# A chunked RWKV-7 scan: transition matrices and corrected receptances made ahead of the chain, y evicted once for four chunks

## The chip, the cores and the metric

One core of one Trainium2 chip. The engines are TensorE (PE, with its weight loads as PEld), VectorE (DVE), ScalarE (ACT), GpSimd (POOL) and SyncE (SP), which here only issues DMAs. The metric is the device time of one launch in microseconds (us), as the median of several runs.

## The reference, cut to what matters

The program is a two-layer trunk over 1280 tokens (a prompt of 256 and a sample of 1024) with 1024 channels. Layer 0 mixes tokens by a bidirectional RWKV-7 recurrence, layer 1 by neighbourhood attention, and each is followed by an MLP. The change is in the recurrence of layer 0 alone, which runs for 16 heads of 64 channels, forwards and backwards, and whose two results are added:

```python
def step(S, inp):
    r_t, w_t, k_t, v_t, a_t, b_t = inp
    sa = jnp.einsum('bhvk,bhk->bhv', S, a_t)
    S = S * w_t[:, :, None, :] + sa[..., None] * b_t[:, :, None, :] + v_t[..., None] * k_t[:, :, None, :]
    return S, jnp.einsum('bhvk,bhk->bhv', S, r_t)
...
for d in range(2):
    ...
    y = y + _wkv_scan(rf, _heads(decay), k_d, vf, -kk, kk * iclr, reverse=(d == 1))
```

Behind it y is normalised per token and head, scaled, given a bonus term, gated and projected.

## The kernel before, in words

**Stages.** The kernel first makes the projections and the scaled operands of the scan (`l0_proj`, `prep_*`), which it stores in DRAM as `ar_d` (a and r), `bk_d` (b and k) and `v_d`. Then comes the scan, then layer 0's output and MLP, attention, and layer 1's MLP. All products of the scan are in float32; all others that matter for the time are split into two float32r halves.

**Chunks.** The scan works in chunks of 64 tokens. Two heads lie side by side in the 128 partitions, so every small product is issued by `pair` (L971) as two 64x64 products, one for each half of the array. A pair whose output lies in the partitions that its operands lie in is called straight here; one whose output goes to the other half (`half(1 - e)`) is called crossed.

**Jobs.** A job is 16 chunks of one pair of heads (the sample), or four chunks of each of four pairs (the prompt, in the first two of the ten jobs). It is scanned forwards (d = 0) and backwards (d = 1) at once, so in each of 16 time units a job makes one step for each direction. Its chunks are prepared in eight groups of four (`order` in `scan_job`), one group each two units.

**Preparation of a job**, in this order, with times in units of the job:
- `load`, `prod`, `store` (L798 to L820): a group's `ar` and the b half of `bk` come in, one product gives the matrix `zb` (PSUM tile aps), DVE masks it (L813), and its left half goes to DRAM (`dd`, L816).
- `mload`, `mtr`, `rank1`, `qst`, `qld` (L823 to L889): the diagonal 32x32 blocks of all 32 matrices of the job come back (`mt`, `mraw`, L831), ACT transposes half of them (L840), DVE inverts them all together by 31 rank-1 updates of two instructions (L851, L853), and the result goes to DRAM (`qd`, L864 and L868) and back into `Q` (the program's name is qq, L884) and `qx` (L889). The updates are put over ten units, by an estimate of their cost.
- `merge1`, `merge2` (L895 to L910): the 64x64 inverses are completed from the 32x32 ones (PSUM tiles yps and qps, ACT copies to yt and qq).
- `kload`, `kprod`, `kmask`, `ktr` (L913 to L942): `bk` comes in, one product and DVE's mask (L926) give `zk`, and two transposes per chunk (PSUM tile lps) give `lt`.

**A step of the chain** (`scan_step`, L976) is four pieces at t - 0.68, t, t + 0.33 and t + 0.66. The state S of the chunk before enters a product into w, ACT copies that to `up` (L993), a product with Q gives u, which ACT copies too (L1007), a product with u completes the new state, and ACT scales that by the decay into the new S (L1015). Beside it three products make the chunk's y in the PSUM tile yo, which DVE copies or adds into y after each step (L1019, L1021). So the chain of a step is three products and three copies on ACT. For each direction there is one bank with w, u and the new state (wu) and one for yo.

**After the steps** of a group pair, `scan_post` normalises y, adds the bonus, transposes (PSUM tile zps) and stores it.

**Order.** PE, DVE, ACT and POOL run in an order written out by hand: each piece of work is put in a list with its time (`at`), and the list is sorted. An engine's instructions are then issued in that order, and an instruction that waits holds up all behind it on its engine. SP's DMAs follow an order that the framework makes, near to that of the list; a DMA that waits holds up those behind it as well. A job's preparation starts at `T0` = -34 units, so two further jobs are being prepared while one is scanned: rank-1 updates of the next job run beside the steps of this one.

**Rings.** 20 buffers each of `ar` and `zb` (10 in pool er, which is opened early, and 10 in rp), 4 of bb, 3 each of `bk`, `zk` and `lt`, and 4 PSUM banks (tag aps) that all the prepared products share.

Of the kernel before, what the change touches and what calls it, by code (L numbers as in the profile page):

```python
# [13 lines left out]
P = 128  # L14
# [34 lines left out]
class Trunk:  # L49
# [654 lines left out]
    def scan_begin(self):  # L704
# [9 lines left out]
                                           (("bb", 4, L), ("ar", 10, P), ("zb", 10, P)))  # L714
# [17 lines left out]
    def scan(self):  # L732
# [12 lines left out]
        grow(self.r_ar, rp, "ar", [P, 4, P], 10)  # L745
        grow(self.r_zb, rp, "zb", [P, 4, P], 10)
# [5 lines left out]
        self.pbank = [[self.pw.tile([P, n], F32, name=f"{x}{d}") for x, n in (("wu", 3 * L), ("yo", L))] for d in range(2)]  # L752
# [26 lines left out]
    def scan_job(self, j):  # L779
# [4 lines left out]
        J = {"ar": {}, "zb": {}, "zk": {}, "lt": {}}  # L784
# [3 lines left out]
        T0 = -34.0  # L788
# [4 lines left out]
        for n, (d, g) in enumerate(order):  # L793
# [78 lines left out]
        def qld():  # L872
# [6 lines left out]
            for d in range(2):  # L879
                for b in range(2):  # L880
                    o = 64 * d + 32 * b
                    for e in range(2):
                        q0 = 64 * e + 32 * b
                        nc.sync.dma_start(Q[q0:q0 + 32, :, d, 32 * b:32 * b + 32], J["qd"][d, o:o + 32].rearrange("(c e) s t -> e s c t", e=2)[e])  # L884
# [7 lines left out]
        for n, (d, g) in enumerate(order):  # L892
            m, c0 = grp[g]

            def merge1(d=d, g=g):  # L895
                zb, qx, lo = J["zb"][d, g], J["qx"][d], 32 * d
                yps = self.pt.tile([P, 4, 32], F32, name="yps", tag="aps")
                for c in range(4):
                    self.pair(lambda e, z: (yps[z, c, :], zb[z, c, 0:64], qx[z, 4 * g + c, :]))
                yt = J["yt", d, g] = self.nxt(self.r_yt[d])  # L900
                nc.scalar.copy(yt[:, :, lo:lo + 32], yps)

            def merge2(d=d, g=g):
                Q, yt, hi = J["Q"], J["yt", d, g], 32 - 32 * d
                qps = self.pt.tile([P, 4, 32], F32, name="qps", tag="aps")
                for c in range(4):
                    self.pair(lambda e, z: (qps[z, c, :], yt[z, c, :], Q[z, 4 * g + c, d, hi:hi + 32]))
                nc.scalar.copy(Q[:, 4 * g:4 * g + 4, d, hi:hi + 32], qps)
            t = 2 * n - 3.992
            at(t + 0.52, merge1)  # L910
            at(t + 1.30, merge2)

# [4 lines left out]
            def kprod(c, d=d, g=g):  # L917
                bk, ar = J["bk", d, g], J["ar"][d, g]
                if c == 0:
                    J["pk"] = self.pa.tile([P, 4, P], F32, name="kps", tag="aps")  # L920
                ps = J["pk"]
                self.pair(lambda e, z: (ps[z, c, :], bk[z, c, 64:128], ar[z, c, :]))

            def kmask(d=d, g=g, ps=None):
                zk = J["zk"][d, g] = self.rp.tile([P, 4, P], F32, name="zk", tag="zk", bufs=3)
                nc.vector.tensor_tensor(out=zk, in0=J["pk"], in1=self.mask[d].unsqueeze(1).to_broadcast([P, 4, P]), op=ALU.mult)  # L926

            def ktr(c, d=d, g=g):
                bk = J["bk", d, g]
                if c == 0:  # L930
                    J["pl"] = self.pt.tile([P, 4, 2, L], F32, name="lps", tag="aps")
                ps = J["pl"]
                for i in range(2):
                    self.pair(lambda e, z: (ps[z, c, i, :], bk[z, c, 64 * i:64 * i + 64], self.ident[z, z]))
                if c == 3:
                    lt = J["lt"][d, g] = self.rp.tile([P, 4, 2, L], F32, name="lt", tag="lt", bufs=3)
                    nc.scalar.copy(lt, ps)
            at(t - 1.9, kload)
            at(t + 1.25, kmask)
# [13 lines left out]
        at(-5.423, vload)  # L953
# [5 lines left out]
        for d in range(2):  # L959
            for i in range(16):  # L960
# [4 lines left out]
                self.scan_step(at, i + 0.481 * d, J, st[d], d, cc, m, c0 + cc % 4, new, end, i >= 8, j == len(self.jobs) - 1 and i == 15)  # L965
# [10 lines left out]
    def scan_step(self, at, t, J, st, d, cc, m, ch, new, end, second, last):  # L976
        nc = self.nc
        g, c = cc // 4, cc % 4
        R = {}
        w, us, sn, yo = (lambda i=i, s=s: self.pbank[d][i][:, s] for i, s in ((0, slice(0, L)), (0, slice(L, 2 * L)), (0, slice(2 * L, 3 * L)), (1, slice(0, L))))  # L980
        half = self.half

        def s0():
            zk, vt = J["zk"][d, g], J["vt"]
            self.pair(lambda e, z: (w()[z], zk[z, c, 0:64], vt[z, 0, cc, :]))

        def s1():
            ar, zk, vt = J["ar"][d, g], J["zk"][d, g], J["vt"]
            S = R["S"] = None if new else st["S"]
            if S is not None:  # L990
                self.pair(lambda e, z: (w()[z], ar[z, c, 0:64], S[z]), start=False, free=True)
            up = R["up"] = self.sp.tile([P, L], F32, name="up", tag="up", bufs=4)
# [900 lines left out]
```

## Time and profile before

| | |
|---|---|
| median of 3 runs | 4080.2 us (4078.45 to 4082.55) |
| the profiled execution | 4085.58 us |
| its span | 4083.8 us |
| granted TensorE clock, mean | 0.964 |
| projections and preparation, 0 to 650 us | PE busy 585.08, DVE 409.66, ACT 416.04 us |
| passage to the scan, 650 to 738 us | PE busy 59.73, DVE 30.48, ACT 15.32 us |
| the scan's steps, 738 to 1409 us | PE busy 569.74, DVE 418.31, ACT 354.46 us |
| all behind it, 1409 to 4083 us | PE busy 2619.65, DVE 1430.70, ACT 772.97 us |

The profile is one execution taken apart: each engine's instructions with their start and duration, named by the line of the kernel and by tiles (out<-in). A busy time is the union of an engine's instructions. Matmuls overlap, so a busy PE can still have room; how close together its products start tells more. Records of PE come twice for each product of the scan: a float32 product runs as two. A window of the trace is given in us from the span's start.

### The profile page before, as it was taken

How to read it: one execution, taken by the hardware profiler on the slowest of the kernel's cores; microseconds unless marked ns; L12 is line 12 of the kernel's file. 1: busy time of each engine (PE TensorE's matmuls, PEld its weight loads, DVE VectorE, ACT ScalarE, POOL GpSimd, SP SyncE). 2: the span in 40 equal slices, each digit the busy share in tenths (PEclk: the TensorE clock that was granted, in tenths of full speed). 3: DMA queues.
4: the chain of work that ended last, by engine and by line, in shares of the span. 5: the costliest groups of instructions: out<-in, count | busy, mean ns of one | idle time of the engine just before them, and what ended most of it. 6: DMA issues, size and time to landing. Idle time of an engine off the chain costs nothing.

```text
span 4083.8 us, 91125 instructions
## 1 busy us (share of the span) xinstructions
PE 3834.2 (94%) x36820; PEld 3242.4 (79%) x36820; DVE 2289.2 (56%) x4861; ACT 1558.8 (38%) x3788; POOL 1336.7 (33%) x1252
## 2 busy tenths in 40 slices
PE   8989988788888799999999999999989999999999
PEld 5765577787878688888888889887778888888888
DVE  5778743566665547555555563355554755555555
ACT  6776641455555432111111133466563211111111
POOL 4446542022221334222222242244442422222222
PEclk9987889899999899999999999999999999999999
DMA  4226564766664331111101115445454111111101
GB/s 140 72 99 223 197 215 119 163 155 160 154 161 112 122 125 42 37 36 42 38 35 42 40 45 172 114 107 113 94 157 167 44 37 37 42 37 37 42 32 63
DMA packets 450886, 394.90 MB, mean 97 GB/s; under 512 B 267456, under 2 KB 352832, under 8 KB 450464
## 3 DMA queue, kind: packets, MB, share of 16 engines
q1 hardware_dynamic: 416048, 327.72, 28.5%
q10 hardware_dynamic: 34416, 61.35, 4.2%
q8 instruction: 289, 4.73, 0.5%
q14 instruction: 133, 1.09, 0.1%
HBM read 270.50 MB, written 124.44 MB: 97 GB/s over the span
## 4 chain that ended last, share of the span: by engine, by line
PE 77%; DVE 9%; ACT 5%; DMA 4%; issue 3%; POOL 2%; SPq 1%; ACTq 0%; DVEq 0%; POOLq 0%
PE ps L95 19%; PE ps L96 18%; PE ps L97 18%; PE wu L974 3%; DVE q L853 2%; PE vps L510 1%; PE vps L512 1%; PE vps L511 1%; DVE tmp L851 1%; PE op L1808 1%; PE aps L974 1%; PE pt L1751 1%; PE kps L974 1%; PE lps L974 1%; PE yo L974 1%
## 5 line engine op out<-in xcount | busy, mean ns | idle before, releaser
L1354 DVE TENSOR_TENSOR x<-ps,x 128x256 f32<-128x256 f32 x1488 | 815.0, 595 | 644.0 <-PE ps L97 643.9
L95 PE MATMUL ps<-ah,whi 128*128 128x512 f32 (+1 forms) x2304 | 842.8, 366 | 0.0
L96 PE MATMUL ps<-al,whi 128*128 128x512 f32 (+1 forms) x2304 | 826.6, 359 | 0.0
L97 PE MATMUL ps<-ah,wlo 128*128 128x512 f32 (+1 forms) x2304 | 822.7, 357 | 1.8 <-DVE wlo L90 1.5
L90 POOL TENSOR_TENSOR wlo<-raw,whi 128x1024 fp32r<-128x1024 f32 (+1 forms) x178 | 390.2, 2192 | 849.6 <-ACT whi L89 821.9
L95 PE MATMUL ps<-hh,whi 128*128 128x512 f32 (+1 forms) x1536 | 547.4, 356 | 9.4 <-DVE x L1354 9.4
L96 PE MATMUL ps<-hl,whi 128*128 128x512 f32 (+1 forms) x1536 | 546.1, 356 | 0.0
L97 PE MATMUL ps<-hh,wlo 128*128 128x512 f32 (+1 forms) x1536 | 545.5, 355 | 0.0
L95 PEld LDWEIGHTS ps<-ah,whi 128*128 128x128 f32 x2304 | 434.4, 189 | 72.9 <-issue 8.1
L97 PEld LDWEIGHTS ps<-ah,wlo 128*128 128x128 f32 x2304 | 433.5, 188 | 72.6 <-DVE wlo L90 2.0
L96 PEld LDWEIGHTS ps<-al,whi 128*128 128x128 f32 x2304 | 434.7, 189 | 61.9 <-issue 1.0
L89 ACT CAST whi<-raw 128x1024 fp32r<-128x1024 f32 (+1 forms) x206 | 200.4, 973 | 708.7 <-PE ps L96 630.2
L1333 POOL TENSOR_TENSOR rl<-rl 128x512 f32<-128x512 f32 (+1 forms) x192 | 174.2, 907 | 506.1 <-PE ps L97 462.5
L95 PEld LDWEIGHTS ps<-hh,whi 128*128 128x128 f32 x1536 | 291.1, 190 | 53.7 <-DVE x L1354 11.4
L97 PEld LDWEIGHTS ps<-hh,wlo 128*128 128x128 f32 x1536 | 291.4, 190 | 41.7
L96 PEld LDWEIGHTS ps<-hl,whi 128*128 128x128 f32 x1536 | 291.2, 190 | 40.6
L1332 ACT ACTIVATE rl<-ps 128x512 f32<-128x512 f32 (+1 forms) x192 | 100.7, 525 | 555.8 <-PE ps L97 555.8
L1335 ACT CAST hh<-rl 128x512 fp32r<-128x512 f32 (+1 forms) x192 | 105.6, 550 | 323.6 <-POOL rl L1333 323.6
L1336 DVE TENSOR_TENSOR hl<-rl,hh 128x512 fp32r<-128x512 f32 (+1 forms) x192 | 119.8, 624 | 143.1 <-ACT hh L1335 142.6
L1745 POOL TENSOR_TENSOR s<-s,mx 128x384 f32<-128x384 f32 (+1 forms) x150 | 109.5, 743 | 163.3 <-DVE mx L1744 113.6
L1050 POOL TENSOR_TENSOR y<-y,mu 128x512 f32<-128x512 f32 x18 | 20.3, 1125 | 372.5 <-DVE mu L1047 292.0
L974 PE MATMUL aps<-ar,bb 64*64 64x128 f32 x1280 | 119.1, 291 | 24.3 <-DMA ar<-ar_d 19.8
(301 smaller groups left out, 8305.8 us busy)
## 6 DMA issues: line engine op xcount, KB each, us to landing
raw<-in_w_down_dram SPq DMA_DIRECT2D x64, 512.0 KB
raw<-in_w_up_dram SPq DMA_DIRECT2D x64, 512.0 KB
ar<-ar_d SPq DMA_DIRECT2D x80, 256.0 KB
bk<-bk_d SPq DMA_DIRECT2D x80, 256.0 KB
ar_d<-ar ACTq DMA_DIRECT2D x32, 512.0 KB
bk_d<-bk ACTq DMA_DIRECT2D x32, 512.0 KB
bs<-tab SPq DMA_DIRECT2D x128, 96.0 KB
v_d<-vt ACTq DMA_DIRECT2D x80, 128.0 KB
```

The lines of the kernel that those rows point to most:

```text
L89: nc.scalar.copy(hi[:, cs], raw)
L90: lo_eng.tensor_tensor(out=lo[:, cs], in0=raw, in1=hi[:, cs].bitcast(F32), op=ALU.subtract)
L95: mm(ps, sh, mh, start=first, stop=False)
L96: mm(ps, sh, ml, start=False, stop=False)
L97: mm(ps, sl, mh, start=False, stop=last)
L974: self.nc.tensor.matmul(out, w, x, start=start, stop=stop, skip_group_check=free)
L1332: nc.scalar.activation(r[:, :n], ps[:, :n], AF.Relu)
L1333: nc.gpsimd.tensor_tensor(out=r[:, :n], in0=r[:, :n], in1=r[:, :n], op=ALU.mult)
L1335: nc.scalar.copy(hh[:, :n], r[:, :n])
L1336: nc.vector.tensor_tensor(out=hl[:, :n], in0=r[:, :n], in1=hh[:, :n].bitcast(F32), op=ALU.subtract)
L1354: nc.vector.tensor_tensor(out=xv, in0=ps[:, :n], in1=xv, op=ALU.add)
L1745: nc.gpsimd.tensor_tensor(out=s[:, :nk], in0=s[:, :nk], in1=mx[:, 2:3].to_broadcast([P, nk]), op=ALU.mult)
```

## The change

The change takes the inverse out of the chain. For each group it makes ahead of time, with S the state before a chunk:
- X = the transposed a half of `ar` beside zk times v, both crossed into the other half's partitions (`turn`, PSUM tile xps, program's name xs);
- U = the inverse times X (`solve`, PSUM tile ups, us): its left half says how u follows from S, its right half is the part of u that doesn't depend on S;
- F = U's left half times b, and times zb's right half (`step`, PSUM tile tps, fs): what S adds to the next state and to y by way of u.

Each is four pairs of 128 columns, or eight of 64, with one copy on ACT for a group. A unit of the chain (`scan_step`) is then up to four terms, v, U, S with the identity, and S with F. Each term is one straight pair into the state's bank (sn) and one crossed pair into yo, issued in turn. Only the two with S depend on the step before, and they are followed by one scaled copy on ACT. w, up and u, with their copies, are gone. Eight steps (four units, two directions) share a bank of yo, of which there are two, and DVE copies or adds it into y once for these, 128x512, in place of eight times 128x64.

Moved: merge1's product is crossed now and issued in turn with kprod's (`keys`); Q is loaded into the other half's partitions; `ktr` is split in two, each issued in turn with X's products; prod and solve are issued in turn, as they have the same time. `T0` is -35.25 in place of -34; the chunks' second preparation starts at T0 + 30.65 + 2n; loads of ar are at 1.5 units ahead of prod and those of bk at 1.6 ahead of their use (before 1.614 and some 2.7). er has 12 each of ar and zb and rp 8; zk and lt have four buffers; the gate's raw tile has five in place of seven.

On PE, in the middle of a job, one direction's step before (wu: w, u and the new state; aps: prod of another group):

```order
L974 MATMUL wu0_7206<-S_14479,ar18_7182 64x64 x2
L974 MATMUL yo0_7207<-v0_7167,zk_14243 64x64 x2
L974 MATMUL aps_14506<-ar15_7179,bb3_6167 64x128 x2
L974 MATMUL wu1_7208<-u_14498,lt_14112 64x64 x2
L974 MATMUL yo1_7209<-u_14498,zb17_7191 64x64 x2
L974 MATMUL aps_14506<-ar15_7179,bb3_6167 64x128 x2
L974 MATMUL wu0_7206<-v0_7167,zk_14243 64x64 x2
L974 MATMUL yo0_7207<-S_14479,ar18_7182 64x64 x2
L974 MATMUL wu0_7206<-v0_7167,lt_14321 64x64 x2
L974 MATMUL wu0_7206<-S_14479,cst_60 64x64 x2
L974 MATMUL wu0_7206<-up_14511,qq0_7169 64x64 x2
L974 MATMUL aps_14506<-ar15_7179,bb3_6167 64x128 x2
```

Here the two directions' pieces (wu0, wu1) and the next group's prod alternate, and each answer of ACT (S, u, up) is waited for in between. On PE at the like place of the change, one unit of the backward direction, and the start of solve (ups) and prod (aps):

```order
L1005 MATMUL sn1_7207<-v1_7172,lt_13568 64x64 x2
L1005 MATMUL yo1_7209<-v1_7172,zk_13499 64x64 x2
L1005 MATMUL sn1_7207<-us_13604,lt_13568 64x64 x2
L1005 MATMUL yo1_7209<-us_13604,zb11_6191 64x64 x2
L1005 MATMUL sn1_7207<-S_13866,cst_60 64x64 x2
L1005 MATMUL yo1_7209<-S_13866,ar11_6179 64x64 x2
L1005 MATMUL sn1_7207<-S_13866,fs_13679 64x64 x2
L1005 MATMUL yo1_7209<-S_13866,fs_13679 64x64 x2
L1005 MATMUL ups_13995<-xs_13965,qq0_7173 64x128 x2
L1005 MATMUL aps_13998<-ar9_6177,bb1_6165 64x128 x2
L1005 MATMUL ups_13995<-xs_13965,qq0_7173 64x128 x2
L1005 MATMUL aps_13998<-ar9_6177,bb1_6165 64x128 x2
```

A unit stands in one piece now, straight (sn, aps) and crossed (yo, ups) pairs in turn. On SP, before, from the end of a job's rank-1 updates on (qd: the inverses on their way out, qq and qx on their way in; dd: zb's halves on their way out):

```order
L864 DMA qd_14249<-q_13180 128x1024
L868 DMA qd_14249<-qt_14248 128x1024
L884 DMA qq1_7170<-qd_14249 32x16x32 x4
L889 DMA qx01_7211<-qd_14249 32x16x32 x2
L884 DMA qq1_7170<-qd_14249 32x16x32 x4
L889 DMA qx11_7223<-qd_14249 32x16x32 x2
L816 DMA dd_13166<-zb14_7188 128x4x64
L915 DMA bk_14515<-bk_d_3253 128x512
L800 DMA ar16_7180<-ar_d_3252 128x512
L816 DMA dd_13167<-zb15_7189 128x4x64
```

And on SP in the change, at the same place:

```order
L865 DMA qd_14993<-q_13796 128x1024
L900 DMA bk_15373<-bk_d_3253 128x512
L885 DMA qq1_7174<-qd_14993 32x16x32
L869 DMA qd_14993<-qt_14992 128x1024
L1101 DMA z_d_6160<-zt_15069 128x256 x2
L885 DMA qq1_7174<-qd_14993 32x16x32 x3
L890 DMA qx01_7211<-qd_14993 32x16x32 x2
L885 DMA qq1_7174<-qd_14993 32x16x32 x4
L890 DMA qx11_7223<-qd_14993 32x16x32 x2
L817 DMA dd_13781<-zb14_7188 128x4x64
L801 DMA ar16_7182<-ar_d_3252 128x512
L817 DMA dd_13782<-zb15_7189 128x4x64
```

The second qd, which feeds the first qx, has moved behind the first load of qq, which reads the first qd; the z stores have moved in between, and one bk has moved ahead.

The diff's core (line numbers are those of after in the profile after):

```diff
-        T0 = -34.0
+        T0 = -35.25
...
-            at(t - (1.614 if j else 7.0), load, E)
+            at(t - (1.5 if j else 7.0), load, E)
             for c in range(5):
-                at(t + (c * 0.133 + -0.013 if c < 4 else 0.577), lambda c=c, f=prod: f(c), E)
-            at(t + (1.263 if j else 1.011), store, E)
+                at(t + 0.07 * c, lambda c=c, f=prod: f(c), E)
+            at(t + 1.1, store, E)
...
-                        q0 = 64 * e + 32 * b
+                        q0 = 64 * (1 - e) + 32 * b
...
+            def keys(c, d=d, g=g):
...
+                self.pair(lambda e, z: (pk[z, c, :], bk[z, c, 64:128], ar[z, c, :]))
+                self.pair(lambda e, z: (py[half(1 - e), c, :], zb[z, c, 0:64], qx[z, 4 * g + c, :]))
...
+            def turn(c, i, d=d, g=g):
...
+                self.pair(lambda e, z: (pl[z, c, i, :], bk[z, c, 64 * i:64 * i + 64], self.ident[z, z]))
+                if i == 0:
+                    self.pair(lambda e, z: (px[half(1 - e), c, 0:64], ar[z, c, 0:64], self.ident[z, z]))
+                else:
+                    self.pair(lambda e, z: (px[half(1 - e), c, 64:128], J["zk"][d, g][z, c, 0:64], J["vt"][z, 0, 4 * g + c, :]))
+                    if c == 3:
...
+                        nc.scalar.copy(X, px)
...
+                        nc.scalar.copy(lt, pl)
+
+            def solve(c, d=d, g=g):
...
+                self.pair(lambda e, z: (ps[z, c, :], Q[half(1 - e), 4 * g + c, d, :], X[half(1 - e), c, :]))
+                if c == 3:
...
+                    nc.scalar.copy(U, ps)
+
+            def step(c, d=d, g=g):
...
+                self.pair(lambda e, z: (ps[z, c, 0:64], U[z, c, 0:64], lt[z, c, 0, :]))
+                self.pair(lambda e, z: (ps[z, c, 64:128], U[z, c, 0:64], zb[z, c, 64:128]))
                 if c == 3:
...
+                    nc.scalar.copy(F, ps)
+            t = T0 + 30.65 + 2 * n
+            at(t - 1.6, kload)
+            at(t + 0.30, kmask)
             for c in range(4):
-                at(t + c * 0.11 + 0.80, lambda c=c, f=kprod: f(c))
-                at(t + c * 0.11 + 1.53, lambda c=c, f=ktr: f(c))
+                at(t + 0.07 * c, lambda c=c, f=keys: f(c))
+                at(t + 0.45 + 0.035 * c, lambda c=c, f=turn: f(c, 0))
+                at(t + 0.72 + 0.035 * c, lambda c=c, f=merge2: f(c))
+                at(t + 0.86 + 0.035 * c, lambda c=c, f=turn: f(c, 1))
+                at(T0 + 2 * n + 32 + 0.07 * c, lambda c=c, f=solve: f(c))
+                at(t + 1.95 + 0.07 * c, lambda c=c, f=step: f(c))
...
-        at(-5.423, vload)
+        at(-7.4, vload)
...
+        def unit():
...
+            terms = [(lambda z: lt[z, c, 1, :], lambda z: zk[z, c, 64:128], lambda z: v[z, 0, cc, :]),
+                     (lambda z: lt[z, c, 0, :], lambda z: zb[z, c, 64:128], lambda z: U[z, c, 64:128])]
             if S is not None:
...
+                terms += [(lambda z: self.ident[z, z], lambda z: ar[z, c, 64:128], lambda z: S[z]),
+                          (lambda z: F[z, c, 0:64], lambda z: F[z, c, 64:128], lambda z: S[z])]
+            for k, (ws, wy, x_) in enumerate(terms):
+                if not end:
+                    self.pair(lambda e, z: (sn[z], ws(z), x_(z)), start=k == 0, stop=k == len(terms) - 1)
+                self.pair(lambda e, z: (yo[half(1 - e), x, c, :], wy(z), x_(z)), start=k == 0 and d == 0 and i % 4 == 0, free=True)
             if not end:
...
+                nc.scalar.activation(S2, sn, AF.Copy, scale=self.dall[:, m, d, ch:ch + 1])
+            if d == 1 and i % 4 == 3:
...
+                if i < 8:
+                    nc.vector.tensor_copy(y, yo)
+                else:
+                    nc.vector.tensor_tensor(out=y, in0=yo, in1=y, op=ALU.add)
+        at(t, unit)
```

More of the change, by code (lines that the diff above doesn't have):

```diff
@@ L750, in scan @@
         self.pw = self.sctx.enter_context(tc.tile_pool(name="pw", bufs=1, space=PSUM))
[L752 removed]
+        self.sbank = [self.pw.tile([P, L], F32, name=f"sn{d}") for d in range(2)]
+        self.ybank = [self.pw.tile([P, 2, 4, L], F32, name=f"yo{i}") for i in range(2)]
         self.r_qx, self.r_yt = [[[], 0], [[], 0]], [[[], 0], [[], 0]]
@@ L893, in scan_job @@
             m, c0 = grp[g]
[L895 to L911, printed above, removed]
+            half = self.half
             def kload(d=d, g=g, m=m, c0=c0):
@@ L930, in ktr @@
                 if c == 0:
[L931 to L934, printed above, removed]
+                    J["pp"] = self.pt.tile([P, 4, P], F32, name="tps", tag="aps")
+                ps = J["pp"]
+                self.pair(lambda e, z: (ps[z, c, 0:64], U[z, c, 0:64], lt[z, c, 0, :]))
+                self.pair(lambda e, z: (ps[z, c, 64:128], U[z, c, 0:64], zb[z, c, 64:128]))
@@ L964, in scan_job @@
                 end = grp[0][1] == 0 and i % 4 == 3 or i == 15
-                self.scan_step(at, i + 0.481 * d, J, st[d], d, cc, m, c0 + cc % 4, new, end, i >= 8, j == len(self.jobs) - 1 and i == 15)
+                self.scan_step(at, i + 0.481 * d, J, st[d], d, cc, m, c0 + cc % 4, new, end, i)
         self.scan_post(at, J, grp, j == len(self.jobs) - 1)
@@ L974, in pair, with scan_step @@
             self.nc.tensor.matmul(out, w, x, start=start, stop=stop, skip_group_check=free)
[L976 removed]
+    def scan_step(self, at, t, J, st, d, cc, m, ch, new, end, i):
         nc = self.nc
         g, c = cc // 4, cc % 4
[L979 to L989, printed above, removed]
[L990 to L1025 removed]
```

92 lines of the change are left out of this document (43 added, 49 removed).

## The prediction

> **What bounds the kernel now.** I took the page, then cut the span into stretches with the busy times by window, then asked for the lines, waits, chain and order in time of one job of the scan. Only the scan changes, so its pace is the question. The first fence has a job's two stretches and the end of the scan (columns: us, then busy time and instructions of PE, PEld, DVE, ACT, POOL, clock, DMA share, GB/s); the second is the same view for line 853 alone, the second half of each rank-1 update.
>
> ```profile
> span 4083.8 us, 91125 instructions
> 1134.20:1174.50 40.30, 36.46 (x1223) 34.50 (x1220) 34.65 (x101) 19.79 (x78) 8.20 (x10) 0.96 0.59 147
> 1174.50:1202.20 27.70, 23.08 (x732) 21.55 (x728) 9.37 (x28) 16.72 (x59) 6.59 (x9) 0.94 0.67 161
> 1307.20:1386.70 79.50, 67.65 (x2348) 61.66 (x2344) 27.59 (x83) 46.97 (x186) 22.09 (x23) 0.99 0.34 96
> 1386.70:1409.00 22.30, 8.57 (x88) 8.32 (x89) 13.80 (x19) 4.82 (x9) 11.59 (x9) 0.51 0.23 78
> ```
> ```profile
> 866.00:1202.20 336.20, 62.41 (x155) 0.97 0.64 156
> 1134.20:1174.50 40.30, 12.48 (x31) 0.96 0.59 147
> 1174.50:1202.20 27.70, 0.00 (x0) 0.94 0.67 161
> ```
>
> Five jobs (155 updates, 31 each) take 336.2 us: 67.2 us a job of 16 time units. A job has two stretches: R, with the 31 rank-1 updates of the next job on DVE (10 units, 40.3 us here), and the link C (6 units, 27.7 us) from the last update to the next job's first. They are limited differently. In R, DVE is busy 34.65 and PE 36.46 of 40.30 us, and the two wait for each other (lines of DVE, then waits, both of R):
>
> ```profile
> L853 DVE TENSOR_TENSOR q<-q,tmp 128x31 f32<-128x31 f32 (+15 forms) x31 | 12.5, 403 | 1.1
> L851 DVE TENSOR_TENSOR tmp<-mt,q 128x60 f32<-128x60 f32 (+15 forms) x30 | 11.4, 382 | 0.4
> L1019 DVE COPY y<-yo 128x64 f32<-128x64 f32 x16 | 3.5, 218 | 0.9 <-PE wu L974 0.9
> L813 DVE TENSOR_TENSOR zb<-aps,cst 128x512 f32<-128x512 f32 x5 | 3.4, 686 | 0.2 <-PE aps L974 0.2
> L1021 DVE TENSOR_TENSOR y<-yo,y 128x64 f32<-128x64 f32 x3 | 0.7, 222 | 2.1 <-PE yo L974 2.1
> ```
> ```profile
> ACT u L1007 <- PE wu L974: 8.1, 17, 1.2
> PE yo L974 <- DVE y L1019: 2.8, 5, 0.8
> DVE y L1021 <- PE yo L974: 2.1, 2, 1.1
> ```
>
> C is a chain of transfers in SP's order: q out, Q and qx in, two last stores of zb, mt and mraw in, their transposition, the first update. DVE is busy 9.37 of 27.70 us in it. SP's queue, then the longest pieces of the chain of waits:
>
> ```profile
> 1174.52 0.32 SPq L864 DMA_DIRECT2D qd<-q  x1
> 1177.34 0.32 SPq L868 DMA_DIRECT2D qd<-qt  x1
> 1177.75 2.83 SPq L884 DMA_DIRECT2D qq<-qd  x4
> 1180.67 0.97 SPq L889 DMA_DIRECT2D qx<-qd  x2
> 1181.69 2.59 SPq L884 DMA_DIRECT2D qq<-qd  x4
> 1184.33 2.21 SPq L889 DMA_DIRECT2D qx<-qd  x2
> 1188.22 0.37 SPq L816 DMA_DIRECT2D dd<-zb  x1
> 1189.41 1.24 SPq L831 DMA_DIRECT2D mt<-dd  x2
> 1193.71 1.02 SPq L831 DMA_DIRECT2D mraw<-dd  x2
> ```
> ```profile
> 980.05 3.58 DMA qx<-qd
> 1187.75 5.49 DMA ar<-ar_d
> 1199.71 0.64 ACT mt L840
> 1202.25 0.74 DVE tmp L851
> ```
>
> **The change, part by part.** *The price of a product.* A pair of 64x64 products runs as two waves of two. PE in order of time, in R-like work:
>
> ```profile
> 1001.37 0.28 PE L974 MATMUL wu<-up,qq 64*64 64x64 f32 x4
> 1001.49 0.34 PE L974 MATMUL lps<-cst,bk 64*64 64x64 f32 x6
> 1001.62 0.27 PE L974 MATMUL yo<-v,zk 64*64 64x64 f32 x2
> 1001.66 0.23 PE L974 MATMUL lps<-cst,bk 64*64 64x64 f32 x2
> 1001.72 0.27 PE L974 MATMUL aps<-ar,bb 64*64 64x128 f32 x1
> 1001.83 0.39 PE L974 MATMUL aps<-ar,bb 64*64 64x128 f32 x4
> 1001.97 0.27 PE L974 MATMUL yo<-u,zb 64*64 64x64 f32 x2
> 1002.05 0.28 PE L974 MATMUL aps<-ar,bb 64*64 64x128 f32 x2
> ```
>
> Four waves of lps go from 1001.49 to 1001.72: 0.058 us each, 0.116 a pair. Two waves 128 wide go from 1001.83 to 1002.05: 0.11 each, 0.22 a pair. In between, yo runs twice and delays neither stream. Its pairs are crossed (rows 0 to 63 of the operands to partitions 64 to 127 of the output), the others straight, and a crossed wave beside a straight one costs nothing here. That is the assumption on which the sum rests.
>
> [...]
>
> *PE in a round* (two units: one group of four chunks prepared, four steps). Before, straight: 24 pairs of steps, 8 transposes, 8 merge pairs, 40 x 0.116 = 4.64, and 8 wide pairs 1.74: 6.4 us. Crossed: 12 of yo, hidden. After, straight: 16 pairs of units, 8 of lps, 4 of merge2, 8 of step, 36 x 0.116 = 4.18, and 8 wide ones (aps, kps) 1.74: 5.9 us. Crossed: 28 pairs 3.25 (16 of yo, 8 of xps, 4 of yps) and 4 wide of solve 0.88: 4.1 us, nearly all issued in turn with straight ones. The two output transposes per round, 0.23, stand alone in both. So the change adds 26% of pairs (78 for 62 with these) and takes 0.5 us off a round, if crossed work is free.
>
> *New waits on PE.* Solve needs X, step needs U, each a 128x512 copy on ACT. The copy of that form, the state's scaled copy (both from the lines of R), and one answer of ACT to PE:
>
> ```profile
> L937 ACT COPY lt<-lps 128x512 f32<-128x512 f32 x5 | 2.9, 586 | 0.2 <-PE lps L974 0.2
> L1015 ACT ACTIVATE S<-wu,dall 128x64 f32<-128x64 f32 x18 | 5.7, 316 | 3.9 <-PE wu L974 2.6 <-PE yo L974 1.3
> ```
> ```profile
> 1001.70 0.21 ACT L1007 COPY u<-wu 128x64 f32<-128x64 f32 x1 [0.55 <-PE wu L974]
> ```
>
> ACT answers wu (1001.37 to 1001.65) at 1001.70, ends at 1001.91, and yo starts at 1001.97: 0.06 us each way. A wait is the last product's 0.27, 0.06, the copy's 0.59 and 0.06: 0.98 us. One unit's products (0.47) lie between, so 0.5 us shows, twice a round. Queued behind it on PE are the next unit and the next group's keys. The chain itself, one product and one scaled copy (0.27 + 0.06 + 0.32 + 0.06, 0.7 us a step), stays far below a round. A round on PE is then 5.9 + 0.23 + 1.0, 7.1 us, and R, five rounds, **35.7 us**.
>
> *DVE in R.* 19 evictions of y (4.2 us) become 2.5 of the form 128x512 (0.69 as zb, 1.7 us): 34.65 - 2.5 = 32.1 us. That is R's lower bound; PE's no-overlap sum is the upper one (rivals). ACT loses up and u (eight of 0.21, 1.7 us a round) and gains X, U, F (three of 0.59, 1.8): still about 20 us in R, no bound. I take PE's 35.7: the waits for X and U lie on the only path. Against 39.5 us, what 67.2 leaves beside C, that is -3.8 in each of 8 jobs: **-30 us**. The first R that has steps beside it has fewer of them: half of that, **-2**.
>
> *C.* SP's order changes: the second store of q now stands behind the first Q load, which waits for the landing of the first store (3.2 us here at most), so it goes 0.4 to 1.5 us later and qx too. A bk load (0.45 us) no longer stands ahead of the last zb store. I take these as equal: C stays 27.7, **0**, bounds -1.5 to +4 a job. PE does not set it: keys wait for qx until 7.2 us (the two qx issues end at 1181.64) + 1 + 3.6, and the 3.1 units from there to the next first update take 11 us, 23 in all. Loads of ar are issued 1.75 units ahead of use (6.2 us at the new pace), against 5.49 us on the worst row: covered, barely; uncovered, 1 us a group.
>
> *End of the scan.* Now 79.5 us. After: 12 us to qx, 16 units at 3.57, 4 at some 1.5 (units alone, with the gate's copies on ACT between): 75. **-4**. The 22.3 us of normalisation behind it stay. Two gate buffers fewer: nothing, the loads have two units of lead.
>
> Sum -36 us. The profiled execution took 4085.6 us (span 4083.8 and 1.8 around it), 5.4 above the median 4080.2. So 4049.6 beside the profile, and **4044 us** for the median.
>
> **The rivals.**
> *DVE sets R.* y no longer ties PE to DVE step by step, so PE may run half a unit ahead, and its waits fall into DVE's time. For it: 2.8 us of PE's waits in R are for y. Then R is 32.5: 8 x -7.0, -56, with the first job and the end -67: **4013 us**. Chance 0.22.
> *Crossed products are not hidden.* The trace shows single crossed pairs, never a steady row of them in turn with straight ones, where four weight loads share 0.058 us. Unhidden, a round gains 4.1 us and R goes to 56: 8 x 16.7 and, for the 8 rounds at the end, 33, less the 4 of there: **about 4240 us, slower**. It decides from the point where R passes 39.5, that is when 0.8 of the 4.1 us (a fifth) shows. Against it: yo's 1.4 us a round today hide so well that straight work (31.9 in R) and 1.2 of transposes leave room for the waits in 40.3. Chance 0.11.
> *The link grows.* The later qx, and ar loads that stand behind it in SP's queue, make C 4 us longer: +32, against -36: **4076 us**, no change. Chance 0.17.
>
> **How the numbers follow.** My forecast has 0.47; 0.03 is left for the unseen. About 0.2% (8 us) is what a measurement here tells from no change. Faster: nearly all of the forecast, DVE's case and a fifth of the link's, 0.72; same 0.13; slower 0.15. The range runs from below DVE's case, with C 1 us shorter, to the link's case and a little of the unhidden products: 4005 to 4085.
>
> **What would show it.** Right: five jobs of updates in about 317 us; R near 36 and C near 28; sn in waves 0.058 us apart with yo between; PE waiting for ACT at ups and tps. DVE's case: R below 33.5, DVE's waits near nothing. Wrong: sn waves 0.11 us apart (crossed not hidden), C above 31 with qx or ar on the chain, or R unchanged.

## The result, and the profile after

After takes 4193.8 us (median; 4189.0 to 4197.2) beside 4079.5 of before: ratio 1.0278, 95% interval 1.026 to 1.0296. It is 114 us **slower**; the forecast was 4044. First the page's span and the queue that brings TensorE's instructions (packets, MB, share), of after, then of before:

```profile
span 4187.2 us, 99857 instructions
q8 instruction: 327, 5.36, 0.5%
```
```profile
q8 instruction: 289, 4.73, 0.5%
```

Next the stretches of after by window, columns as in the prediction: four jobs, one R, one C, the end of the scan from the last update on.

```profile
959.10:1276.40 317.30, 235.31 (x9728) 215.41 (x9728) 178.32 (x400) 149.60 (x377) 61.13 (x72) 0.98 0.56 133
1199.10:1243.00 43.90, 33.75 (x1408) 31.07 (x1411) 37.17 (x87) 19.71 (x52) 11.60 (x13) 1.00 0.56 132
1243.00:1276.40 33.40, 24.61 (x1040) 23.12 (x1031) 7.16 (x13) 17.67 (x43) 3.69 (x5) 0.95 0.62 143
1396.90:1490.00 93.10, 74.15 (x3024) 67.62 (x3020) 20.36 (x39) 46.39 (x122) 16.72 (x18) 1.00 0.27 76
```

317 us, which was to be the time of five jobs, is that of four. R is 43.9 us (40.3 before), C 33.4 (27.7), the end 93.1 (79.5). Over six jobs of the middle R is 45.3 us in the mean for 39.2, C 33.7 for 27.6. Everything is longer, though PE is busy for less of it: 33.75 of R's 43.90 us here, 36.46 of 40.30 before. For whom does PE wait? PE's waits between 760 and 1380 us (us in total, times, longest):

```profile
PE sn L1005 <- issue: 29.6, 31, 2.9
PE ups L1005 <- ACT xs L940: 18.3, 39, 2.0
PE xps L1005 <- ACT fs L963: 16.9, 49, 0.4
```

The first row names no engine: nothing that the profile shows ended these waits. Such rows stand for every tile. In order of time they look like this:

```profile
904.06 0.27 PE L1005 MATMUL kps<-ar,bk 64*64 64x128 f32 x1
904.07 0.23 PE L1005 MATMUL yps<-qx,zb 64*64 64x32 f32 x2
904.10 0.38 PE L1005 MATMUL kps<-ar,bk 64*64 64x128 f32 x3
904.28 0.27 PE L1005 MATMUL lps<-cst,bk 64*64 64x64 f32 x2
906.46 0.21 PE L1005 MATMUL lps<-cst,bk 64*64 64x64 f32 x1 [1.90 <-issue]
906.47 0.27 PE L1005 MATMUL xps<-cst,ar 64*64 64x64 f32 x2
...
907.10 0.23 PE L1005 MATMUL yo<-us,zb 64*64 64x64 f32 x2
907.11 0.26 PE L1005 MATMUL sn<-S,cst 64*64 64x64 f32 x2
907.16 0.23 PE L1005 MATMUL yo<-us,zb 64*64 64x64 f32 x2
907.17 0.26 PE L1005 MATMUL sn<-S,cst 64*64 64x64 f32 x2
907.21 0.23 PE L1005 MATMUL yo<-S,ar 64*64 64x64 f32 x2
907.23 0.26 PE L1005 MATMUL sn<-S,fs 64*64 64x64 f32 x2
```

Two things stand here. The sn waves are 0.058 us apart with a yo wave between each two: the crossed products are hidden in the array, as assumed. And between two transposes of one tile, with data long there, PE does nothing for 1.90 us. The trace's records of that queue explain it: a packet of 16 KB ran from 903.93 to 904.99 us, and PE went on 1.47 us after it. Between 738 and 1522 us there are 134 such gaps of over 0.25 us from one start to the next, 140 us in all; 81% of them end 1.3 to 1.6 us after a packet landed. The count of PE and PEld records from one gap's end to the next is a multiple of 256 or one less in 103 of 133 cases, and two to four less in 28 more (before: 35 gaps, 21 us). The 83368 records of PE and PEld on the page are 255 for each of the queue's 327 packets. So a packet is a **block of 256 instructions**. Where PE has had to wait for a block, the next one is started 1.3 us (median) after PE has begun it, takes 1.1, and can be used 1.4 after it has landed: some 3.8 us a block in the median. A pair is two products of two weight loads and two matmuls each, 8 instructions. By this estimate a round of before, 62 x 8 = 496 instructions or 1.94 blocks, needs 7.4 us of its 8.4; a round of after, 624 or 2.44 blocks, needs 9.3 us of its 9.9. The theory of the supply: **after is held by the number of its instructions**.

### The profile page after: what moved, and what is told of

The parts are those of the page before. It is cut to its first block, busy times and chain, and to the rows that moved or that the text cites. A ratio compares the mean times of both kernels' runs of the same rounds, so it can differ in the third digit from the quotient of the medians.

```text
span 4187.2 us, 99857 instructions
## 1 busy us (share of the span) xinstructions
PE 3837.7 (92%) x41684; PEld 3237.2 (77%) x41684; DVE 2289.7 (55%) x4581; ACT 1574.4 (38%) x3388; POOL 1341.6 (32%) x1252
## 4 chain that ended last, share of the span: by engine, by line
PE 77%; ACT 6%; DVE 5%; issue 5%; DMA 3%; POOL 2%; SPq 1%; ACTq 0%; DVEq 0%; POOLq 0%
PE ps L95 18%; PE ps L96 18%; PE ps L97 18%; PE tps L1005 2%; PE vps L510 2%; PE vps L511 1%; PE vps L512 1%; PE sn L1005 1%; PE xps L1005 1%; PE aps L1005 1%; PE ups L1005 1%; PE yo L1005 1%; PE op L1816 1%; PE kps L1005 1%; PE pt L1759 1%
## 5 line engine op out<-in xcount | busy, mean ns | idle before, releaser
L1025 ACT ACTIVATE S<-sn,dall 128x64 f32<-128x64 f32 x288 | 91.7, 318 | 210.0 <-PE sn L1005 204.8
L814 DVE TENSOR_TENSOR zb<-aps,cst 128x512 f32<-128x512 f32 x80 | 55.0, 688 | 208.9 <-PE aps L1005 175.9
```

## The experiments

The table sums up all runs but before_nop, which stands at the end. Scan is the time from the first to the last scaled state; blocks are the packets started in it; the gaps are PE's idle stretches over 0.1 us with no releaser, all from the profile of each run. Ratios are to before on the same chip.

| run | pairs a round | ratio (95%) | blocks | scan us | gaps us |
|---|---|---|---|---|---|
| before | 62 | 1 | 145 | 642.9 | 13 |
| before_split | 70 | 1.0106 (1.0085-1.0128) | 163 | 685.4 | 88 |
| before_y4 | 62 | 0.9968 (0.9956-0.9981) | 145 | 634.7 | 43 |
| before_y4_lt | 58 | 1.0159 (1.0145-1.0173) | 135 | 710.3 | 1 |
| before_y4_sd | 58 | 0.9991 (0.9982-1.0) | 137 | 638.8 | 10 |
| y4_pool | 62 | 1.0027 (1.0015-1.004) | 145 | 656.3 | 43 |
| after | 78 | 1.0278 (1.026-1.0296) | 182 | 749.5 | 109 |
| after_split | 90 | 1.0506 (1.0481-1.053) | 209 | 851.9 | 183 |
| after_step | 74 | 1.0227 (1.0199-1.0255) | 172 | 733.2 | 94 |
| after_fold | 70 | 1.0176 (1.0149-1.0203) | 165 | 719.5 | 60 |
| after_both | 66 | 1.0122 (1.0108-1.0135) | 155 | 703.0 | 45 |
| after_later | 78 | 1.0296 (1.0282-1.031) | 182 | 771.4 | 151 |
| both_later | 66 | 1.0151 (1.0136-1.0165) | 155 | 704.4 | 75 |
| after_half | 78 | 1.0267 (1.025-1.0285) | 182 | 769.3 | 120 |
| after_noyo | 66 | 1.0126 (1.0108-1.0144) | 154 | 707.8 | 32 |
| noyo_later | 66 | 1.0107 (1.0085-1.0128) | 154 | 695.9 | 68 |
| noyo_later_pool | 66 | 1.0055 (1.0039-1.0071) | 154 | 668.9 | 78 |

**More instructions, the same work.** before_split and after_split make each 128 wide product in two halves (aps and kps; in after also ups).

```diff
-self.pair(lambda e, z: (ps[z, c, :], bb[z, c, :], ar[z, c, :]))
+for h in (slice(0, 64), slice(64, 128)):
+    self.pair(lambda e, z: (ps[z, c, h], bb[z, c, :], ar[z, c, h]))
```


> The kernel before, with the products for aps and kps made as two of 64 columns each: 8 pairs a round more (70 for 62), nothing else. Theory of the supply: 5,120 instructions, 20 blocks; before has 147 blocks in its 671 us of scan, 4.56 us each, so part of the 20 x 4.1 goes into the slack: +45 us, 4125 us (4095 to 4165). Theory of the waits and theory of the crossed products: before's 4080 us, within 10.

> The kernel after, with the 128 wide products for aps, kps and ups each made as two products of 64 columns: 12 pairs a round more (90 for 78), the same columns through the array, the same copies and waits. Theory of the supply (TensorE runs out of instructions: the queue that brings them delivers 256 at a time, one block in some 4.1 us, and a pair is 8 instructions): 12 x 8 x 80 rounds = 7,680 instructions, 30 blocks, +123 us: 4317 us (4270 to 4340), with gaps that nothing in the profile ends after nearly every block. Theory of the waits (the scan is longer because TensorE waits for the copies of X, U and F): 4194 us, within 15. Theory of the crossed products (the crossed products take waves of their own): the array's columns are the same, 4194 us within 15.

1.0106 is 43 us, 45 were expected. After_split is 0.0228 above after, 93 us; 123 were expected, with at least 76. The same columns went through the array, the same copies were waited for, so neither the waits nor the crossed products give this. Nor do the additional weight loads: a wave of aps takes 0.112 us in before and half a wave 0.058 in before_split, a wave of ups 0.109 in after and half of one 0.058 in after_split. From that the array's own price of splitting is, as an estimate, some 5 us of the 43 and at most 13 of the 93. PE's waits of before_split from 760 to 1380 us (before has y's copies on top there, 20.7 us, and 13 us of gaps in its whole scan):

```profile
PE wu L976 <- issue: 28.2, 41, 1.3
PE lps L976 <- issue: 17.7, 15, 2.6
```

**Fewer instructions.** after_step makes F with one product, after_fold adds the identity and ar to F as it is copied, after_both does both.

```diff
-self.pair(lambda e, z: (ps[z, c, 0:64], U[z, c, 0:64], lt[z, c, 0, :]))
-self.pair(lambda e, z: (ps[z, c, 64:128], U[z, c, 0:64], zb[z, c, 64:128]))
+self.pair(lambda e, z: (ps[z, c, :], U[z, c, 0:64], zb[z, c, :]))
...
-nc.scalar.copy(F, ps)
+nc.vector.tensor_tensor(out=F[:, :, 0:64], in0=ps[:, :, 0:64], in1=self.id2.unsqueeze(1).to_broadcast([P, 4, L]), op=ALU.add)
+nc.vector.tensor_tensor(out=F[:, :, 64:128], in0=ps[:, :, 64:128], in1=J["ar"][d, g][:, :, 64:128], op=ALU.add)
```


> The kernel after, with F made by one product of 128 columns a chunk in place of two of 64 (lt's first half is copied into zb's first half, which is free by then, so that both stand side by side): 4 pairs a round fewer (74), one ScalarE copy more, the same columns through the array. Theory of the supply: 2,560 instructions fewer, 10 blocks, -41 us: 4153 us (4140 to 4170). Theory of the waits: the extra copy is in the way or not: 4194 to 4210. Theory of the crossed products: 4194 within 10.

> The kernel after, with the identity and ar's second half added to F as it is copied out (two additions on VectorE in place of one copy on ScalarE), so that a unit of the chain has three terms in place of four: 8 pairs a round fewer (70), 4 of them straight and 4 crossed. Theory of the supply: 5,120 instructions fewer, 20 blocks, -82 us: 4112 us (4090 to 4135). Theory of the waits: at most the 4 straight pairs, 4 x 2 x 0.058 x 80 = 37 us: 4157 to 4194 us, nearer the end without a gain, since F's copy now queues on VectorE. Theory of the crossed products: 8 x 2 x 0.058 x 80 = 74 us: 4120 us; it does not tell itself from the supply by this run.

> The kernel after with both edits, the one product for F and the folding of the identity and ar into F: 66 pairs a round for 78, 154 blocks of instructions for 182. Theory of the supply alone (each block less is 4.1 us less): -115 us, 4079 us. Supply and waits (a block takes the longer of its delivery, 3.7 to 4.1 us, and its own work with the waits in it, so that what the supply gives up the copies of X and U take in part): the two single edits gave 21 and 42 us by their ratios, so 4130 us (4110 to 4150). Theory of the crossed products: 4 x 2 x 0.058 x 80 = 37 us for the crossed ones and at most as much for the straight ones, 4120 to 4157.

21, 42 and 64 us came back: the right sign each time, half of the price. after_fold also takes four straight pairs a round away, so alone it doesn't tell the supply from the array's time. Gaps fell from 109 us in after to 45 in after_both, but a block now took 4.54 us for 4.12: waits came up in their place, those for the copy of X from 22 to 52 us. So the supply alone is not the whole loss.

**The waits.** after_later puts solve 0.45 and step 0.6 units later; both_later is the same on after_both.

```diff
-at(T0 + 2 * n + 32 + 0.07 * c, lambda c=c, f=solve: f(c))
+at(T0 + 2 * n + 32.45 + 0.07 * c, lambda c=c, f=solve: f(c))
-at(t + 1.95 + 0.07 * c, lambda c=c, f=step: f(c))
+at(t + 2.55 + 0.07 * c, lambda c=c, f=step: f(c))
```


> The kernel after, with the products of U 0.45 units later and those of F 0.6 units later, so that the copies of X and U have had time: the instructions are the same, 78 pairs. In the trace of after TensorE stands 53 us for the copies of X (22), F (21) and U (9), and 109 us for nothing. Theory of the waits: most of the 53 us go, 4145 to 4165 us. Theory of the supply: the blocks come no faster, the waits turn into gaps without a releaser, 4180 to 4200 us.

> Both edits (66 pairs a round) and the later products of U and F. Supply and waits: with 154 blocks the waits are what is left over the supply (61 us of them in the run with the identity folded), and moving them gives half of them back: 4095 us (4075 to 4115). Supply alone, waits worth nothing: as after_both. If it falls to 4070 or less, the design is sound and only the instructions were too many.

In after_later the waits for X, U and F fell from 53 us to 4, the gaps rose from 109 to 151, those for VectorE's masks (zb and zk) from 14 to 26, and the time did not fall (1.0296). As long as the supply is the later one, the waits for the copies cost nothing that shows. both_later missed: 1.0151, no better than after_both. There VectorE, on which the fold had put F's additions, was busy 39.1 of R's 42.7 us (mean of six jobs; 34.1 of 38.8 in before). But R was 2 us shorter than in after_both; what grew was C, by 4.4 us a job, along with a change in SP's order that is shown below.

**Only hidden work taken away.** after_noyo keeps of yo's four products the first (`if k == 0`), after_half keeps all of them, three with half the columns (`n`).

```diff
+n = L if k == 0 else 32
...
-    self.pair(lambda e, z: (sn[z], ws(z), x_(z)), start=k == 0, stop=k == len(terms) - 1)
+    self.pair(lambda e, z: (sn[z, 0:n], ws(z), x_(z)[:, 0:n]), start=k == 0, stop=k == len(terms) - 1)
...
+if k == 0:
     self.pair(lambda e, z: (yo[half(1 - e), x, c, :], wy(z), x_(z)), start=k == 0 and d == 0 and i % 4 == 0, free=True)
```


> The kernel after, with three of the four crossed products of a unit's y left out (y then holds the v term alone): 12 pairs a round fewer (66 for 78), all of them crossed, which the trace shows beside straight ones at no time of the array; chain, copies and waits are those of after, and nothing is added to VectorE or ScalarE. Theory of the supply: 28 to 30 blocks fewer at 3.5 to 4.1 us: -100 us, 4095 us (4080 to 4125, 1.000 to 1.011 of before). Theory of the waits: hidden products cost nothing, 4194 us, 1.028. Theory of the crossed products: 12 x 2 x 0.058 x 80 = 111 us, 4083 us; after_half tells it from the supply.

> The kernel after, with three of the four terms of each unit's state and y made for 32 of the 64 columns (the other columns hold the first term alone): every instruction is still there, with half the columns through the array. Theory of the supply: the instructions are as many, 4194 us within 15 (1.024 to 1.031 of before). Theory of the crossed products, or of any in which the array's time sets the pace: straight waves 3 x 4 x 2 x 0.029 x 80 = 56 us, with the crossed ones 111: 4083 to 4138 us (1.001 to 1.014).

Half the columns gave nothing (1.0267, after 1.0278). That test is weaker than planned: in its trace the waves of the U term fell to 0.03 us, but those of the two S terms kept 0.058, so by an estimate from these waves it could have given 17 us at most. Leaving out products that the array hides gave back 62 us (1.0278 to 1.0126); 100 were expected, and SP's order, shown below, may have taken the rest. Then the waits rule; PE from 760 to 1380 us in after_noyo:

```profile
PE ups L1005 <- ACT xs L940: 69.1, 52, 8.3
PE xps L1005 <- ACT fs L963: 20.4, 59, 0.4
```

**Both away, and a third thing.**

> after_noyo (three of the four crossed products of y left out, 66 pairs a round) with the products of U and F 0.45 and 0.6 units later as in after_later. In after_noyo the period of a job is 75.6 us where before has 66.9, and TensorE stands 117 us of the scan for the copies of X, U and F. Theory that supply and waits together are the whole loss: with both taken away the time comes to that of before, 4080 us (4060 to 4100, 0.995 to 1.005 of before). If something third holds the job (the stretch from the last rank-1 update to the next job's first, 33 us where before has 28, by the queue of loads), it stays at 4115 to 4135 (1.008 to 1.013).

It stayed at 1.0107, some 8 us under after_noyo with overlapping intervals. The two were not both away, though: PE's waits for X fell from 73 to 4 us, but those for F stood (27 us, 24 in after_noyo), those for VectorE's masks zb and zk rose from 2 to 29, and the gaps from 32 to 68. So the run doesn't tell what the waits are worth. The time lies in the range that was given for C held by the queue of loads, and C was 32.5 us; this comes back below. VectorE was busy 37.1 of R's 41.9 us (34.1 of 38.8 in before), although y's copies are fewer. Its rows say why: after's VectorE, after's GpSimd, then VectorE in before, with the start, the duration and the shapes:

```profile
1201.20 0.24 DVE L852 TENSOR_TENSOR tmp<-mt,q 128x87 f32<-128x87 f32 x1
1201.47 1.10 DVE L854 TENSOR_TENSOR q<-q,tmp 128x87 f32<-128x87 f32 x1
1202.60 0.80 DVE L852 TENSOR_TENSOR tmp<-mt,q 128x112 f32<-128x112 f32 x1
```
```profile
1201.42 1.04 POOL L1083 TENSOR_TENSOR y<-y,rqr 128x512 f32<-128x512 f32 x1 [4.11 <-ACT us L952]
1202.54 1.44 POOL L1088 TENSOR_TENSOR y<-y,lnx 128x256 f32<-128x256 f32 x2
```
```profile
1204.07 0.25 DVE L853 TENSOR_TENSOR q<-q,tmp 128x87 f32<-128x87 f32 x1
1204.35 0.27 DVE L851 TENSOR_TENSOR tmp<-mt,q 128x112 f32<-128x112 f32 x1
```

An update of 128x87 took 0.25 us alone and 1.10 with GpSimd's step on y beside it. GpSimd is busy 11.6 us a job in R in place of 7.9. That this comes of `T0`, 1.25 units earlier, by which R meets the steps of y's first half as well, is argued; `T0` was not moved by itself. noyo_later_pool moves these steps behind R; y4_pool, below, does it to before_y4.

```diff
+late = ((p3b, 26.1), (p4, 26.2), (p4b, 26.5), (p5, 26.8), (tr, 28.0)), ((p2, 28.1), (p2b, 28.7), (p2c, 29.0), (p3, 29.3),
+        (p3b, 29.7), (p4, 29.8), (p4b, 30.1), (p5, 30.4), (tr, 32.0))
+late = {} if last else {f: x - t0 - 1.25 for f, x in late[half]}
...
-    at(t0 + dt, f)
+    at(t0 + late.get(f, dt), f)
```


> noyo_later with the last steps on y (GpSimd's scaling, weighting and adding, and the turning of y) moved in the order of the engines out of the stretch with the rank-1 updates into the stretch between two jobs. In the trace a rank-1 instruction with a GpSimd operation beside it takes 0.87 us on VectorE, one without 0.33; after has 11.8 us of GpSimd in the stretch where before has 8.0, and the updates take 27.0 us a job for 24.3. Theory of the collision (VectorE's rank-1 updates are the third thing): 4 to 6 us a job come back, 9.5 jobs: 4075 to 4095 us (0.997 to 1.002 of before). If the supply holds the stretch by now (5 rounds of 528 instructions at 3.7 to 4.1 us a block, 38 to 42 us, where it takes 41.9): 4115 to 4132 (1.006 to 1.011).

1.0055, 21 us less: C fell from 32.5 to 29.1 us, R from 41.9 to 40.9, VectorE's part of it from 37.1 to 33.5. It was half of what the theory gave, and most of it is not the collision's: that lies in R, which gave 1.0 us a job, while C gave 3.4. C's part goes with SP's order. SP of noyo_later, then of noyo_later_pool, from the store of q on (... where rows are left out):

```profile
1210.24 0.44 SPq L865 DMA_DIRECT2D qd<-q  x1
...
1224.51 0.98 SPq L817 DMA_DIRECT2D dd<-zb  x2
1225.59 1.18 SPq L900 DMA_DIRECT2D bk<-bk_d  x1
1230.78 0.36 SPq L817 DMA_DIRECT2D dd<-zb  x1
1231.24 1.11 SPq L832 DMA_DIRECT2D mt<-dd  x2
```
```profile
1192.86 1.41 SPq L865 DMA_DIRECT2D qd<-q  x1
...
1208.08 0.40 SPq L817 DMA_DIRECT2D dd<-zb  x1
1208.72 1.85 SPq L832 DMA_DIRECT2D mt<-dd  x2
...
1214.08 1.01 SPq L817 DMA_DIRECT2D dd<-zb  x1
```

In noyo_later the load of mt, with which the next updates begin, stands behind one store of zb more, that of a later job, and SP waits for that matrix: mt goes 21.0 us after q's store, in noyo_later_pool 15.9. Counted by the stores ahead of it, this is so for seven of the ten loads of mt in after_noyo, noyo_later and both_later, for two in after_fold and after_both, for one in noyo_later_pool, and for none in before or after. None of these edits touches the loads; the framework's order moved with them. The last eight stretches C together take 24 us less in noyo_later_pool than in noyo_later, and 30 less than in after_noyo. That is about what after_noyo lacks of the 100 expected; as noyo_later_pool moves y's steps and the stores of z too, it is an estimate of what the order cost. So the collision is seen on single updates, but of its worth in time the runs separate no more than R's 1.0 us a job. With 154 blocks for before's 145, the 0.0055 that remain would fit the nine blocks more, which was not tried.

**Before with parts of the change.** before_y4 evicts y by four chunks and leaves all else.

```diff
-            if not second:
-                nc.vector.tensor_copy(y[:, cc, :], yo())
+            if d == 1 and i % 4 == 3:
...
+                    nc.vector.tensor_copy(y4, yb)
```


> The kernel before with one part of the change alone: y is gathered in two banks and evicted by four chunks of both directions, 8 copies a job for 32; the chain and the instructions of TensorE are those of before. Supply: before's blocks take 4.43 us each where 4.1 is the least seen, so that of the 21 us that TensorE stood for y's copies a part comes back: 4065 us (4055 to 4075). If y's new banks were what made after slower: above 4090. Theory of the crossed products: the same 62 pairs, 4060 to 4080.

0.9968, 13 us faster (15 expected): PE's 21 us of waits for y went, gaps rose from 13 to 43 (25 in before_nop, which has before's instructions). This part of the change is good, and before_y4 is the fastest version found. Three attempts to go on from there failed:

```diff
-    self.pair(lambda e, z: (ps[z, c, i, :], bk[z, c, 64 * i:64 * i + 64], self.ident[z, z]))
+self.pair(lambda e, z: (ps[e][:, c, :], bk[z, c, :], self.ident[z, z]))
```


> before_y4 (y evicted by four chunks), with bk turned by products whose weights are 128 columns wide, both halves of a chunk at once: 4 pairs a round fewer (58 for 62), the two heads in two banks, and 4 copies of half the partitions on ScalarE in place of one. Theory of the supply: 10 blocks fewer, at 4.1 to 4.4 us each at most -41 us; the edits of after kept half of that, so 20 us under before_y4: 0.992 of before (0.985 to 0.997). Against it: three copies a round more on ScalarE, some 1 us that u's copies may queue behind: up to 1.005. If instructions cost nothing: 0.997 to 1.005.

```diff
-self.pair(lambda e, z: (sn()[z], self.ident[z, z], S[z]), start=False, free=True)
+nc.gpsimd.tensor_scalar(out=R["sd"], in0=S, scalar1=self.dall[:, m, d, ch:ch + 1], scalar2=None, op0=ALU.mult)
...
+nc.vector.scalar_tensor_tensor(out=S2, in0=sn(), scalar=self.dall[:, m, d, ch:ch + 1], in1=R["sd"], op0=ALU.mult, op1=ALU.add)
```


> before_y4, with the state's own part added on VectorE (S = sn x decay + S x decay, the second product made on GpSimd beforehand) in place of a product with the identity on TensorE: 4 pairs a round fewer (58 for 62), S made on VectorE and not on ScalarE. Theory of the supply: 10 blocks fewer, 20 to 40 us under before_y4: 0.990 of before (0.983 to 0.997). Against it: S now stands in VectorE's queue between the rank-1 updates, 32 a job; if that costs 0.3 us a unit of the chain, it is 1.00 to 1.02.

> before_y4 with the same move of GpSimd's steps on y. VectorE is busy 35.6 of the 38.3 us of the stretch with the rank-1 updates, of which the collision with GpSimd takes 3 to 4. Theory of the collision: 2 to 4 us a job, 0.987 to 0.992 of before (4030 to 4050 us). If the supply holds the stretch (5 rounds of 496 instructions at 3.7 to 4.0 us a block, 35.8 to 38.8): 0.992 to 0.998.

before_y4_lt turns bk by products of 128 columns of weights, with four copies for one; blocks fell to 135 and gaps to 1 us, but the copies stand ahead of the chain's up on ScalarE, 74 us of PE's waits. before_y4_sd came out 0.0023 above before_y4: VectorE's S cost PE 40 us of waits. y4_pool missed both of its ranges: the move that gave 21 us above cost 24 us here. GpSimd's part of R fell only from 8.1 to 6.7 us, C was 29.4 us for 28.0 and R longer as well, and PE newly waited 17 us for the masks zb and zk; which of these costs the time was not tried. Fewer instructions are no gain where their removal brings such waits.

One run more was to add instructions alone:

```diff
 self.nc.tensor.matmul(out, w, x, start=start, stop=stop, skip_group_check=free)
+self.nc.tensor.nop(nofuse=True)
```


> The kernel before with an empty instruction on TensorE's queue behind each product of the scan: 124 a round beside its 496, 620 in all, nearly the 624 of after; no product, copy or wait more. Theory of the supply: the blocks go from 145 to about 182 and the scan takes what after's takes, +90 to +110 us: 4185 us (4150 to 4200), with gaps that nothing ends after most blocks. If TensorE's own time or the waits decide: 4080 to 4095.

The empty instructions are not in its trace: 91125 instructions and 145 blocks are those of before, and so is the time (0.9996, 0.9985 to 1.0007). So it tells nothing on the supply. As a second trace of the same instructions it tells how far the gaps differ by themselves: 25 us, in before 13.

## Why the prediction was wrong

- **The step that failed** is the round on PE: "So the change adds 26% of pairs (78 for 62 with these) and takes 0.5 us off a round, if crossed work is free." It is free in the array, as the 0.058 us waves show, but not in instructions. Those 26% are 0.5 blocks, 1.9 us a round at 3.8 us a block. before_split, with 8 pairs more and no new work, and after_noyo, with 12 hidden pairs fewer, show that pairs cost time by their number: 43 and 62 us. The sum had a round at 7.1 us; the blocks give 9.3, and the job's 79.3 us by eight are 9.9. Before stood at 7.4 of 8.4 us, so there was room for some 13% more and not for 26.
- **The new waits** (1.0 us a round) were in the trace, 53 us or 0.65 a round, but did not add to the time (after_later). In after_noyo, with fewer instructions, they came up to 117 us.
- **DVE in R** was to fall from 34.65 to 32.1 us and rose to 37.17 in the R above, with GpSimd busy 11.60 us of it (8.20 before). y's evictions fell as said; that the change also moves what lies beside the rank-1 updates was left out. noyo_later_pool separates no more than R's 1.0 us a job for it.
- **C** was taken as unchanged (bounds -1.5 to +4); it grew by 6 us. "PE does not set it" failed: in all six jobs ACT began mt's transposition 30.0 us (mean) after the last update, right behind its copy yt and a wait for PE's product yps. The later qx came as well: the last one was issued 15.3 us after the last update for 12.3 in before, and mraw 23.6 for 20.3. So, as an estimate, some 3 of the 6 us would have come by the loads alone.
- **The end of the scan** took 93.1 us in place of 75: 16 units at PE's pace again.
- **The rivals.** "Crossed products not hidden" has the right sign for the wrong reason: its sign, sn waves 0.11 us apart, did not come; in after's trace the sn waves kept 0.058 us with yo between them. Splitting products that are not crossed costs as much a pair (43 us for 8, against 62 for 12 left out). "The link grows" had the sign C above 31, and it came, with about half of C's growth (estimate) by the later loads and the rest by PE's pace. No rival counted instructions, though the page's q8 row and the 35 gaps of before were there to read.

Of 0.0278, 0.0152 (62 us) goes with twelve hidden pairs a round, in a run in which SP's order cost some 30 us besides, by the estimate above; 0.0052 (21 us) goes with moving y's last steps, most of it in C, where SP's order had changed; 0.0019 with the later U and F is not distinguished from nothing, and 0.0055 is left, with four pairs a round more than before. That the instructions cost time is shown; how the loss divides beyond them stays open.

## What to carry to other kernels

When products are small, count the instructions as well as the time in the array: in after TensorE's gaps that nothing ended came mostly at multiples of 256 instructions, 109 us of them in the scan, and 4 to 12 pairs a round fewer gave 21 to 64 us back; in before_y4_lt four pairs fewer went with waits for ScalarE's copies, and the time rose from before_y4's 0.9968 to 1.0159. Work that hides beside other work in one resource must be asked what it costs in every other. When a piece is moved in a hand-written order, look up what runs beside it on the other engines: here a VectorE update of 0.25 us took 1.10 with a step of GpSimd beside it. And before an edit is read as a test of one thing, compare the order of the DMAs, which can move with it.

## What the runs showed of the hardware

- TensorE's instructions came in blocks of 256, 16 KB each, in after at 3.4 us (the shortest twentieth) to some 4 us a block (median 3.97), about 65 instructions a us, while sn and yo in turn used 8 in 0.058 us. After's scan had 109 us of gaps that nothing in the profile ended.
- In after the 127 VectorE updates that had a GpSimd operation beside them for some of their time took 0.82 us in the median, the 493 others 0.36. Of the second instruction (L854) at 128x87, nine took 1.10 us in the median with one beside them and eleven 0.25 without. In the rows above the update of 1.10 us ends 0.11 us after GpSimd's step beside it.
